# A two-layer hybrid decoder: ScalarE empties some PSUM banks alone, memory values in rows of 512, x transposed block by block in tasks of its own, another first block

## The chip, the cores and the metric

One core of a Trainium2 chip runs the whole program. TensorE (PE in the profile; PEld is its loading of the stationary operand) multiplies into PSUM banks; VectorE (DVE) and ScalarE (ACT) read PSUM and SBUF; GpSimd (POOL) does small work in SBUF; SyncE (SP) only issues DMAs here, one after another. Each engine works through its own instructions in the order in which they stand, and waits on semaphores for the others. The metric is the device time of one execution in microseconds (us), as a median over runs; lower is better.

## The reference

Two layers over x (512 tokens, 1024 wide), all in fp32, cut to its structure:

```python
for l in range(2):
    h = x @ w_in[l]                       # 1024 -> all branches' columns
    y_rwkv = rwkv7(...)                   # 8 heads x 64, delta-rule state, sequential
    q = rms(q_lat) @ w_uq; kv = rms(kv_lat) @ w_ukv
    y_mla = causal_attention(q, k, v) * silu(gate)          # 8 heads, 96 + 64 wide
    u = val * sigmoid(glu); u = causal_conv31(u) + conv_b
    y_conv = silu(layer_norm(u)) * silu(gate)
    kv = mem @ w_mem_kv                   # mem: 256 tokens; keys 512 wide, values 512 wide
    y_mem = attention(xq, k_mem, v_mem) * silu(gate)        # 4 heads x 128
    proj = [y_n @ w_o_branch[l, n] for n in range(4)]
    out = sum(sigmoid(x @ w_gate_n + b_n) * proj_n) @ w_out[l]
    x = layer_norm(alpha * x + out) * ln_g + ln_b
```

## The kernel before

**Three multiplications for one.** Every fp32 operand is split in two: `h`, the value rounded to TensorE's fp32r, and `lo`, the rest. `mm3` makes a product from lo·h, h·h and h·lo. `split(h, lo, src)` is a copy on ScalarE (h) and a subtraction on VectorE (lo), both reading `src`. Where `src` is a PSUM bank, the bank is held until VectorE has subtracted.

**Stages.** x stands transposed, as eight blocks of 128 features x 512 tokens (`xh`, `xl`). Per layer come the latents (`pl`, two items of 336 columns, `lat_item`), then blocks of 128 columns of W_in against all of x (`ps_glu`, `ps_val`, `ps_xq`, `ps_r` and so on, 24 multiplications of 128x512 each), causal attention in four pairs of heads (`pq` and `pk` project a pair, `heads` empties them and sends them by DMA to their places, `ms`, `mt`, `mo` are scores, transposes and sums), the memory attention (`ps_mk` keys, `pmv` values, `xs`, `xt`, `xo`), the convolution (31 taps on VectorE into `cacc`, then `conv_norm`), the RWKV chunks (64x64 multiplications `g`, `x`, `va`, `gb`, `w`, `yb`), and the merge (`ps_m` gates, `po` projections). At the end of layer 0 stand the output projection (`pz`), the LayerNorm per block of 128 tokens (`norm`, tiles `z` with statistics `lmv`, `lrs`, `lnb`), the store of x for later (`xtok`), and the transposes `xT` that make the next layer's x.

**What sets the order.** A planner (class `Plan`) runs when the program is built. It has a cost for each instruction, a clock for each engine, tasks (generators, each with a due time) and a stream of weight-consuming items. It lets a task issue when its time has come on TensorE's clock and otherwise the next piece of the stream; the instructions stand on each engine in the order in which it issued them. A change in one place therefore moves instructions in many others.

**Buffers.** `wr` holds 2 raw weight blocks (512 KB each), `wh`/`wl` 3 split ones; the DMA of a block is issued once the raw block two before it is split. PSUM has pools of 2 banks for projections (`pp`), 2 for transposes and small products (`pa`), 4 for the rest (`pg`).

**Between the layers.** `ORDER` lists the items: `z0` (512 columns of the output projection), `z2`, `z3` (256 each), `m0` to `m3` (keys of layer 1's memory) and `m4`, `m5` (its values, 256 columns each: 48 multiplications of 128x256). After the fourth `norm` one task goes over the eight blocks of x: four transposes into a `pa` bank, ScalarE's scale and shift into `xf`, ScalarE's copy `xh`, VectorE's `xl`; then the next block.

**The start.** SP issues x's block 0, the first two weight blocks, the other blocks of x. TensorE starts once block 0 of x and the whole first weight block are split, with the product that needs the latest part (`w0l`).

Of the kernel before, what the change touches and what calls it, by code (L numbers as in the profile page):

```python
# [24 lines left out]
U_SLOTS = 32  # L25
ORDER = ["z0", "m0", "m1", "z2", "m2", "m4", "z3", "m3", "m5"]
LOOK = 4
# [238 lines left out]
def trunk_kernel(ctx: ExitStack, tc: tile.TileContext, A, out, dbg=None):  # L266
# [163 lines left out]
    wlive = {"raw": 0, "hl": {}}  # L430

    def weights(name, src, parts, last=False):
# [29 lines left out]
        plan.spawn(run(), plan.done[raw.tensor.name][0])  # L462
        return ws

    def free(h):
        n = h.tensor.name
        wlive["hl"][n] -= 1
        if wlive["hl"][n] == 0:
            del wlive["hl"][n]

# [28 lines left out]
    def wide(get, ps, lhs, wait=None):  # L499

        for k in range(8):
# [3 lines left out]
            for b in range(len(ps)):  # L505
                xh, xl = lhs(k, b)
                mm3(ps[b], xh, xl, h, lo, k == 0, k == 7)
                if b % 2 and (k < 7 or b < 3):
                    yield
# [45 lines left out]
    def memory_items(l):  # L555
# [19 lines left out]

        def keep(x, i, b, ps):
            h, lo = (y[:, 256 * b:256 * b + 256] for y in res[x][i])
            return split(h, lo, ps)

        def keys(h):  # L580
            def run(get):
                ps = yield from project(get, ms, f"mk{h}_{l}", 256)
                yield from keep("k", h // 2, h % 2, ps)
                yield
            return run

        def vpart(b):
            def after(i, ps):
                yield from keep("v", i, b, ps)
                if b == i == 1:  # L590
                    MEM[l] = (res["k"], res["v"])
                yield

            def run(get):
# [4 lines left out]
        its += [([(A["w_mv"][l, b, kh], (512, 512)) for kh in range(2)], vpart(b)) for b in range(2)]  # L599
        return load, its, lambda: len(ms) == 8  # L600

    def layer_items(l):
# [28 lines left out]
        if l == 0:  # L631
            x0 = [u(f"x0{k}") for k in range(8)]
            DMA(x0[0], A["xT"][:, 0, :])

        def begin(get):
            if l == 0:
                def loads():
                    for k in range(1, 8):
                        if k == 4:
# [509 lines left out]
        def conv_norm():  # L1149
            ntok = []  # L1150
            yield lambda: added[3] == 8
            for tb in range(4):
                ps, = yield from pa.take([128, 512], f"ct{tb}" + t_)
                for i in range(4):
                    TR(ps[:, 128 * i:128 * i + 128], cacc[i][:, 128 * tb:128 * tb + 128])
                yield
                bs, mv = st(f"cbs{tb}" + t_, 6), st(f"cmv{tb}" + t_, 2)
                V.bn_stats(bs, ps)
                V.bn_aggr(mv, bs)
                rs = st(f"crs{tb}" + t_, 1)  # L1160
                rstd_of(rs, mv[:, 1:2], 1.0, LN_EPS)
                n = u(f"cn{tb}" + t_)
# [108 lines left out]
        def lat_item(nb):  # L1271
            def run(get):
# [5 lines left out]
                for k in range(8):  # L1278
                    h, lo = yield from get()
                    yield from part(X[l], k)  # L1280
                    for tb in range(4):
                        xh, xl = (x[:, 128 * tb:128 * tb + 128] for x in X[l][k])
                        mm3(ps[tb], xh, xl, h, lo, k == 0, k == 7)
                        if tb % 2:
                            yield
                    free(h)
# [346 lines left out]
        def end_items():  # L1633
# [148 lines left out]
            def norm(tb):  # L1782
# [31 lines left out]
                for k in range(8):  # L1814
                    ps, = yield from pa.take([128, 512], f"xT{k}" + t_)
                    plan.due(*[z[tb][k // 4] for tb in range(4)])
                    yield
                    for tb in range(4):
                        TR(ps[:, 128 * tb:128 * tb + 128], z[tb][k // 4][:, 128 * (k % 4):128 * (k % 4) + 128])
                    yield  # L1820
                    f = u(f"xf{k}" + t_)
                    h = xp.tile([128, 512], F32R, tag="xh", name=f"xh{k}_{l + 1}")
                    lo = xp.tile([128, 512], F32R, tag="xl", name=f"xl{k}_{l + 1}")
                    S.activation(f, ps, AF.Identity, scale=pr("ln_g", k), bias=pr("ln_b", k))
                    pa.free()
                    S.copy(h, f)
                    V.tensor_tensor(out=lo, in0=f, in1=h.bitcast(F32), op=ALU.subtract)
                    X[l + 1].append((h, lo))
                close_phase()
                closed[l] = True  # L1830

# [137 lines left out]
def layout(x, mem, positions, w_in, b_gate, rwkv_mu, rwkv_w0, rwkv_w2, rwkv_a0, rwkv_a2, rwkv_k_k, rwkv_k_a,  # L1969
# [29 lines left out]
    a["w_mk"] = np.stack([tiles(xattn_w_mem_kv[l][:, :512], 128, 8)[:, 0] for l in range(L)])  # L1999
    a["w_mv"] = np.stack([tiles(xattn_w_mem_kv[l][:, 512:], 256, 4) for l in range(L)])  # L2000
    a["w_o"] = np.stack([[tiles(w_o_branch[l, n], 128, 4)[:, 0].reshape(4, 2, 128, 512).transpose(0, 2, 1, 3).reshape(4, 128, 1024)
# [34 lines left out]
```

## Time and profile before

| | us |
|---|---|
| median of 3 runs (lowest, highest) | 1505.58 (1505.47, 1506.05) |
| profiled execution: its own time | 1506.66 |
| profiled execution: span of the core | 1504.9 |
| PE busy in the span | 1474.2 |
| DVE busy | 1053.5 |
| ACT busy | 662.1 |
| POOL busy | 137.1 |
| first multiplication starts, last one ends | 6.75, 1494.66 |
| mean granted TensorE clock over the span | 0.996 |

A busy engine is an engine with an instruction in flight; since multiplications overlap, PE busy says how long TensorE was occupied, not that it ran at its peak. Rows of a timeline have the start and length in us, the engine, the operation, what it writes and reads, and in brackets the idle time of the engine before it and what ended it.

### The profile page before, as it was taken

To read this page: it belongs to the slowest core of one execution; us is meant where nothing else is said; L and a number is where in the kernel's file an instruction comes from. 1 tells how busy PE (TensorE), PEld (TensorE's weight loads), DVE (VectorE), ACT (ScalarE), POOL (GpSimd) and SP (SyncE) were. 2 spreads that over 40 slices of the span, in tenths; PEclk is the share of its full clock that TensorE was granted. 3 is DMA by queue.
4 is the path that set the end of the run, shared out by engine and by line. 5 is a ranking of instruction groups with operands and counts; after the bars stand their busy time and mean duration, and the time that the engine had idled before them with its cause. 6 is when DMAs were issued, how large, how long until landed. Compare 5 with 4: busy or idle time off the path is not lost.

```text
span 1504.9 us, 29132 instructions
## 1 busy us (share of the span) xinstructions
PE 1474.2 (98%) x11896; PEld 1239.7 (82%) x11896; DVE 1053.5 (70%) x1994; ACT 662.1 (44%) x1270; POOL 137.1 (9%) x329
## 2 busy tenths in 40 slices
PE   8999999999999999999999999999999999999997
PEld 8888878888888888888998878888887788888886
DVE  5799997755757666645554888887876476757747
ACT  5546554434354543443255455533444344444332
POOL 0000000030303030000010000000030203021002
PEclk9999999999999999999999999999999999999998
DMA  6444333241322323434343252423332313233532
GB/s 213 124 136 108 86 100 96 84 111 59 86 83 78 91 74 95 136 103 129 114 147 108 82 138 68 116 92 99 88 95 72 97 47 107 63 107 116 165 99 70
DMA packets 89013, 153.50 MB, mean 102 GB/s; under 512 B 41008, under 2 KB 47152, under 8 KB 88880
## 3 DMA queue, kind: packets, MB, share of 16 engines
q1 hardware_dynamic: 88880, 151.65, 33.9%
q8 instruction: 93, 1.52, 0.4%
q14 instruction: 40, 0.33, 0.1%
HBM read 134.32 MB, written 5.77 MB: 93 GB/s over the span
## 4 chain that ended last, share of the span: by engine, by line
PE 90%; DVE 5%; ACT 2%; issue 1%; DMA 1%; POOL 0%; SPq 0%; ACTq 0%; POOLq 0%; DVEq 0%
PE ps_m L286 23%; PE po L286 11%; PE ps_xq L286 3%; PE ps_v L286 3%; PE ps_xg L286 3%; PE ps_cg L286 3%; PE ps_rg L286 3%; PE ps_k L286 3%; PE ps_mg L286 3%; PE ps_r L286 3%; PE ps_val L286 3%; PE ps_glu L286 2%; PE ms L286 2%; PE pl L286 2%; PE pz L286 2%; PE pmv L286 2%
## 5 line engine op out<-in xcount | busy, mean ns | idle before, releaser
L235 DVE SCALAR_TENSOR_TENSOR cacc<-hpad,prm,cacc 128x512 f32<-128x512 f32 x240 | 179.2, 749 | 3.9
L235 ACT ACTIVATE tm<-ps_m,prm 128x512 f32<-128x512 f32 x64 | 44.1, 689 | 166.6 <-PE ps_m L286 156.1
L235 DVE SCALAR_TENSOR_TENSOR mt<-tm,po 128x512 f32<-128x512 f32 x48 | 32.9, 686 | 89.9 <-PE po L286 89.6
L235 POOL TENSOR_TENSOR tmpW<-ZT,W 64x14 f32<-64x14 f32 (+6 forms) x112 | 42.7, 381 | 7.8
L235 POOL TENSOR_TENSOR ZT<-ZT,tmpW 64x14 f32<-64x14 f32 (+6 forms) x112 | 42.0, 375 | 8.8
L235 ACT ACTIVATE mP<-ms,nmm 128x128 f32<-128x128 f32 (+3 forms) x64 | 33.6, 529 | 20.3 <-DVE nmm L235 19.5
L235 POOL TENSOR_SCALAR ZT<-W 64x256 f32<-64x256 f32 x8 | 3.6, 447 | 369.7 <-DMA W<-scr 369.7
L235 ACT COPY mPT<-mt 128x128 f32<-128x128 f32 (+3 forms) x64 | 26.1, 428 | 19.6 <-PE mt L291 19.4
L235 DVE TENSOR_TENSOR merged<-merged,mt 128x512 f32<-128x512 f32 x48 | 33.6, 699 | 1.7
L235 POOL MEMSET D<- 128x8 f32 x8 | 0.9, 116 | 342.7 <-PE ms L286 321.2
L235 DVE TENSOR_REDUCE nmm<-ms 128x1 f32<-128x128 f32 (+3 forms) x64 | 30.0, 484 | 0.1
L235 POOL TENSOR_SCALAR lrs<-lmv 128x1 f32<-128x1 f32 x8 | 3.6, 447 | 253.6 <-DVE lmv L235 252.2
L235 DVE TENSOR_SCALAR mP<-mP,smm 128x128 f32<-128x128 f32 (+3 forms) x64 | 24.8, 387 | 2.3
L291 PE MATMUL mt<-cst,mP 128*128 128x128 f32 x160 | 25.9, 273 | 0.0
L235 DVE SCALAR_TENSOR_TENSOR merged<-tm,po 128x512 f32<-128x512 f32 x16 | 11.0, 687 | 20.1 <-PE po L286 20.0
L235 ACT ACTIVATE z<-z,lnb,lrs 128x256 f32<-128x256 f32 (+1 forms) x16 | 9.6, 647 | 30.1 <-DVE lnb L235 30.1
L235 POOL TENSOR_SCALAR gr<-gm 128x8 f32<-128x8 f32 x8 | 2.4, 298 | 224.0 <-DVE gm L235 224.0
L235 ACT ACTIVATE yb<-yb,mr,gr 128x64 f32<-128x64 f32 x64 | 22.1, 434 | 1.1 <-DVE mr L235 1.1
L286 PE MATMUL ms<-kTl,qT 96*128 96x128 f32 (+3 forms) x64 | 22.3, 348 | 0.0
L291 PEld LDWEIGHTS mt<-cst,mP 128*128 128x128 f32 x160 | 19.0, 141 | 3.6 <-ACT xP L235 0.2
L235 ACT ACTIVATE xP<-xs,nmx 128x256 f32<-128x256 f32 x32 | 15.1, 473 | 13.7 <-DVE nmx L235 11.2
L286 PE MATMUL ms<-kTh,qT 96*128 96x128 f32 (+3 forms) x64 | 20.6, 322 | 0.0
(3536 smaller groups left out, 5276.3 us busy)
## 6 DMA issues: line engine op xcount, KB each, us to landing
w<-in_w_ch_dram SPq DMA_DIRECT2D x146, 512.0 KB, 3.8
w<-in_w_o_dram SPq DMA_DIRECT2D x32, 512.0 KB, 3.7
w<-in_w_out_dram SPq DMA_DIRECT2D x16, 512.0 KB, 3.7
w<-in_w_lat_dram SPq DMA_DIRECT2D x16, 336.0 KB, 3.2
w<-in_w_mk_dram SPq DMA_DIRECT2D x8, 512.0 KB, 3.7
w<-in_w_mv_dram SPq DMA_DIRECT2D x8, 512.0 KB, 3.7
w<-in_w_qk_dram SPq DMA_DIRECT2D x8, 320.0 KB, 2.9
x<-in_xT_dram SPq DMA_DIRECT2D x8, 256.0 KB, 5.9
```

The costliest lines, as they stand in the source:

```text
L235: return self.plan.keep(f(*a, **k))
L286: plan.keep(nc.tensor.matmul(o, lhsT, rhs, start=start, stop=stop))
L291: plan.keep(nc.tensor.transpose(o, i, ident))
```

## The change

1. `ORDER` loses `m5`: the values of layer 1's memory are one item of 512 columns (`m4`) behind `z3` and `m3`; layer 0 has the same item. `w_mv` is laid out for it.
2. Eighteen multiplications of 128x256 on a constant (`warm`) stand first on TensorE; nothing reads them.
3. The first weight block comes in two DMAs and is split in two halves, and blocks 1 and 2 of x are issued ahead of the second weight block. For block 0 the products of the first four banks are issued h·h, then l·h, then h·lo.
4. `heads`: ScalarE copies the bank to SBUF with the scale; `split` then reads SBUF.
5. `conv_norm`: ScalarE copies the bank to SBUF, statistics and normalisation read that; the second affine is done on ScalarE.
6. Between the layers each block of x is a task of its own (`features`), so that two are under way in the two `pa` banks.

```diff
-ORDER = ["z0", "m0", "m1", "z2", "m2", "m4", "z3", "m3", "m5"]
+ORDER = ["z0", "m0", "m1", "z2", "m2", "z3", "m3", "m4"]
...
+    warm = pp.tile([128, 512], F32, tag="pp", name="warm")
+    for i in range(18):
+        MM(warm[:, 0:256], reset[:, 0:128], reset, start=True, stop=True)
...
-        DMA(raw, src)
+        first = name == "w0"
+        if first:
+            for i in range(2):
+                c = slice(parts[0] * i, parts[0] * i + parts[0])
+                DMA(raw[:, c], src[:, c], f"w0{i}")
+            for k in range(1, 3):
+                DMA(x0[k], A["xT"][:, k, :])
+        else:
+            DMA(raw, src)
...
-            if last:
+            if last or first:
                 for i, (w, c) in enumerate(zip(ws, parts)):
+                    if first:
+                        plan.t = max(plan.t, plan.done[f"w0{i}"][0])
+                        yield
...
-        def vpart(b):
...
-                return narrow(get, 256, 2, f"pmv{b}{l}", lambda k, i: [x[:, 128 * i:128 * i + 128] for x in ms[k]], after)
-            return run
+        def values(get):
+            ps = [pp.tile([128, 512], F32, tag="pp", name=f"pmv{i}_{l}") for i in range(1 + (l > 0))]
+            if l == 0:
+                ps += yield from pa.take([128, 512], f"pmv1_{l}")
+            yield from wide(get, ps, lambda k, b: [x[:, 128 * b:128 * b + 128] for x in ms[k]])
+
+            def after():
+                for i in range(2):
+                    yield from keep("v", i, slice(0, 512), ps[i])
+                if l == 0:
+                    pa.free()
+                MEM[l] = (res["k"], res["v"])
+            plan.spawn(after())
+            yield
...
                 yield
+                n = u(f"cn{tb}" + t_)
+                S.copy(n, ps)
+                pa.free()
                 bs, mv = st(f"cbs{tb}" + t_, 6), st(f"cmv{tb}" + t_, 2)
-                V.bn_stats(bs, ps)
+                V.bn_stats(bs, n)
...
-                V.tensor_scalar(out=n, in0=ps, scalar1=mv[:, 0:1], scalar2=rs, op0=ALU.subtract, op1=ALU.mult)
-                pa.free()
+                V.tensor_scalar(out=n, in0=n, scalar1=mv[:, 0:1], scalar2=rs, op0=ALU.subtract, op1=ALU.mult)
...
-                V.tensor_scalar(out=z, in0=ps, scalar1=pr("cln_g", i), scalar2=pr("cln_b", i), op0=ALU.mult, op1=ALU.add)
+                S.activation(z, ps, AF.Identity, scale=pr("cln_g", i), bias=pr("cln_b", i))
...
+                    if l == nb == k == 0:
+                        for a, b in ((0, h), (1, h), (0, lo)):
+                            for tb in range(4):
+                                MM(ps[tb], X[l][k][a][:, 128 * tb:128 * tb + 128], b, start=a == 0 and b is h, stop=False)
...
-            S.activation(parts[0], ps, AF.Copy, scale=s)
-            V.scalar_tensor_tensor(out=parts[1], in0=ps, scalar=s, in1=parts[0].bitcast(F32), op0=ALU.mult, op1=ALU.subtract)
+            raw = parts[1].bitcast(F32)
+            S.activation(raw, ps, AF.Copy, scale=s)
+            yield from split(*parts, raw)
...
+                    plan.spawn(features(k, [z[tb][k // 4][:, 128 * (k % 4):128 * (k % 4) + 128] for tb in range(4)]))
```

**How rows move.** First place: SP's queue at the start of the program (x00 to x07 are the blocks of x, w0 to w3 the first weight blocks). Before:

```order
L298 DMA x00_104<-in_xT_dram 128x512
L298 DMA w0_113<-in_w_lat_dram 128x672
L298 DMA w1_115<-in_w_lat_dram 128x672
L298 DMA x01_105<-in_xT_dram 128x512
L298 DMA x02_106<-in_xT_dram 128x512
L298 DMA x03_107<-in_xT_dram 128x512
```

and now:

```order
L298 DMA x00_123<-in_xT_dram 128x512
L298 DMA w0_132<-in_w_lat_dram 128x336 x2
L298 DMA x01_124<-in_xT_dram 128x512
L298 DMA x02_125<-in_xT_dram 128x512
L298 DMA w1_137<-in_w_lat_dram 128x672
L298 DMA x03_126<-in_xT_dram 128x512
```

The first weight block is two transfers, and the second one moved behind blocks 1 and 2 of x; x04 to x07, w2 and w3 follow as before.

Second place: ScalarE between the layers, behind the third token block's LayerNorm (`z20`). Before:

```order
L235 ACTIVATE z30_0_7314<-z30_0_7314,lnb3_0_8430,lrs3_0_8400 128x512
L235 CAST kmh1_1_7802<-ps_mk3_1_8406 128x256
L235 ACTIVATE xf0_0_8458<-xT0_0_8434,prm0_194 128x512
L235 CAST xh0_1_8459<-xf0_0_8458 128x512
L235 CAST w126h_8471<-w126_8407 128x1024
L235 ACTIVATE xf1_0_8479<-xT1_0_8464,prm0_194 128x512
L235 CAST xh1_1_8480<-xf1_0_8479 128x512
```

and now:

```order
L235 ACTIVATE z30_0_7296<-z30_0_7296,lnb3_0_8346,lrs3_0_8316 128x512
L235 CAST kmh1_1_7784<-ps_mk3_1_8322 128x256
L235 CAST w124h_8380<-w124_8323 128x1024
L235 ACTIVATE xf0_0_8383<-xT0_0_8368,prm0_224 128x512
L235 CAST xh0_1_8384<-xf0_0_8383 128x512
L235 ACTIVATE xf1_0_8388<-xT1_0_8369,prm0_224 128x512
L235 CAST xh1_1_8389<-xf1_0_8388 128x512
```

The copy `kmh1` of the last key bank still stands behind `z30`; w126, which was the second of the two last value blocks, is now the last of four (w123 to w126), and w124's copy stands ahead of x's first block.

Third place: ScalarE at the last pair of heads of layer 0 (`pq3`, `pk3` are its banks). Before:

```order
L235 CAST w34h_2226<-w34_2224 128x1024
L235 ACTIVATE xqh_0_2258<-pq3_0_2237 128x512
L235 ACTIVATE xP21_0_2202,smx211_0_2247<-xs21_0_2201,nmx211_0_2246 128x256
L235 CAST w35h_2271<-w35_2269 128x1024
L235 ACTIVATE xkh_0_2274<-pk3_0_2254 128x512
```

and now:

```order
L235 CAST w34h_2230<-w34_2228 128x1024
L235 COPY xy2_0_2262<-xo2_0_2253 128x512
L235 ACTIVATE xql_0_2269<-pq3_0_2241 128x512
L235 CAST xqh_0_2268<-xql_0_2269 128x512
L235 CAST w35h_2280<-w35_2278 128x1024
L235 ACTIVATE xkl_0_2284<-pk3_0_2264 128x512
L235 CAST xkh_0_2283<-xkl_0_2284 128x512
```

The bank is read by one ScalarE instruction (`xql<-pq3`), in the place where `xqh` stood; the copy behind it and VectorE's subtraction read SBUF.

More of the change, by code (lines that the diff above doesn't have):

```diff
@@ L460, in run @@
             wlive["raw"] -= 1
-        plan.spawn(run(), plan.done[raw.tensor.name][0])
+        plan.spawn(run(), plan.done["w00" if first else raw.tensor.name][0])
         return ws
@@ L507, in wide @@
                 mm3(ps[b], xh, xl, h, lo, k == 0, k == 7)
-                if b % 2 and (k < 7 or b < 3):
+                if b % 2 and (k < 7 or b < len(ps) - 1):
                     yield
@@ L574, in load, with keep @@
                     ms.append((h[:, c], lo[:, c]))
[L576 to L577 removed]
+        def keep(x, i, c, ps):
+            h, lo = (y[:, c] for y in res[x][i])
             return split(h, lo, ps)
@@ L582, in run @@
                 ps = yield from project(get, ms, f"mk{h}_{l}", 256)
-                yield from keep("k", h // 2, h % 2, ps)
+                yield from keep("k", h // 2, slice(256 * (h % 2), 256 * (h % 2) + 256), ps)
                 yield
             return run
-        def vpart(b):
[L588 to L594, printed above, removed]
-                return narrow(get, 256, 2, f"pmv{b}{l}", lambda k, i: [x[:, 128 * i:128 * i + 128] for x in ms[k]], after)
-            return run
+        def values(get):
[11 more added lines that the diff above has]
+            yield
         its = [([(A["w_mk"][l, h], (512, 512))], keys(h)) for h in range(4)]
-        its += [([(A["w_mv"][l, b, kh], (512, 512)) for kh in range(2)], vpart(b)) for b in range(2)]
+        its += [([(A["w_mv"][l, i], (512, 512)) for i in range(4)], values)]
         return load, its, lambda: len(ms) == 8
@@ L631, in layer_items @@
         if l == 0:
-            x0 = [u(f"x0{k}") for k in range(8)]
+            x0.extend(u(f"x0{k}") for k in range(8))
             DMA(x0[0], A["xT"][:, 0, :])
@@ L637, in loads @@
                 def loads():
-                    for k in range(1, 8):
+                    for k in range(3, 8):
                         if k == 4:
@@ L1814, in norm, with features @@
                 for k in range(8):
[L1815 to L1830, printed above, removed]
+                    plan.spawn(features(k, [z[tb][k // 4][:, 128 * (k % 4):128 * (k % 4) + 128] for tb in range(4)]))
+            def features(k, zs):
+                ps, = yield from pa.take([128, 512], f"xT{k}" + t_)
+                plan.due(*zs)
+                yield
+                for tb in range(4):
+                    TR(ps[:, 128 * tb:128 * tb + 128], zs[tb])
+                yield
+                f = u(f"xf{k}" + t_)
+                h = xp.tile([128, 512], F32R, tag="xh", name=f"xh{k}_{l + 1}")
+                lo = xp.tile([128, 512], F32R, tag="xl", name=f"xl{k}_{l + 1}")
+                S.activation(f, ps, AF.Identity, scale=pr("ln_g", k), bias=pr("ln_b", k))
+                pa.free()
+                yield from split(h, lo, f)
+                while len(X[l + 1]) < k:
+                    yield lambda: len(X[l + 1]) == k
+                X[l + 1].append((h, lo))
+                if k == 7:
+                    close_phase()
+                    closed[l] = True
             if l + 1 < LAYERS:
@@ L1999, in layout @@
     a["w_mk"] = np.stack([tiles(xattn_w_mem_kv[l][:, :512], 128, 8)[:, 0] for l in range(L)])
-    a["w_mv"] = np.stack([tiles(xattn_w_mem_kv[l][:, 512:], 256, 4) for l in range(L)])
+    a["w_mv"] = np.stack([tiles(xattn_w_mem_kv[l][:, 512:], 512, 2)[0] for l in range(L)])
     a["w_o"] = np.stack([[tiles(w_o_branch[l, n], 128, 4)[:, 0].reshape(4, 2, 128, 512).transpose(0, 2, 1, 3).reshape(4, 128, 1024)
```

22 lines of the change are left out of this document (13 added, 9 removed).

## The prediction

> **What bounds the kernel now.** I read the page's busy times and its chain of work that ended last, then the waits of TensorE, then the timeline at the places that the change touches.
>
> ```profile
> PE 1474.2 (98%) x11896; PEld 1239.7 (82%) x11896; DVE 1053.5 (70%) x1994; ACT 662.1 (44%) x1270; POOL 137.1 (9%) x329
> PE 90%; DVE 5%; ACT 2%; issue 1%; DMA 1%; POOL 0%; SPq 0%; ACTq 0%; POOLq 0%; DVEq 0%
> ```
>
> TensorE is busy for 98% of the span and carries 90% of the chain. So an edit can save time in three ways only: fewer or better shaped rows on TensorE, a higher clock for them, or a shorter wait of TensorE. Its waits, longest sum first (total us, times, longest), say how much there is:
>
> ```profile
> PE pl L286 <- DVE w0l L235: 6.7, 1, 6.7
> PE pmv L286 <- DVE w126l L235: 2.6, 1, 2.6
> PE tk L291 <- DVE S L235: 1.8, 1, 1.8
> PE pq L286 <- DVE xql L235: 1.6, 2, 0.9
> PE ps_xq L286 <- DVE xql L235: 1.4, 2, 0.9
> PE ps_glu L286 <- DVE xql L235: 1.1, 1, 1.1
> PE gb_0x L286 <- issue: 1.1, 1, 1.1
> ...
> PE ps_mg L286 <- DVE xql L235: 0.6, 1, 0.6
> PE gb_1x L286 <- issue: 0.6, 1, 0.6
> PE pz L286 <- DVE w123l L235: 0.6, 1, 0.6
> PE ps_val L286 <- DVE w11l L235: 0.5, 1, 0.5
> ```
>
> Three groups of these waits are edited: the head (w0l, 6.7), the heads' banks (xql, 1.6 + 1.4 + 1.1 + 0.6 = 4.7) and the place between the layers (w126l, w123l, 3.2). The other four rows (1.8 + 1.1 + 0.6 + 0.5 = 4.0) are not touched, but a re-planned order can move them.
>
> **The head.** Timeline and window of the start:
>
> ```profile
> 0.72 0.48 POOL L235 MEMSET reset<- 128x256 bf16 x2 [0.29 <-POOLq L2028]
> 5.05 0.75 ACT L235 CAST w0h<-w 128x672 fp32r<-128x672 f32 x1 [0.27 <-DMA w<-in_w_lat_dram]
> 6.75 0.65 PE L286 MATMUL pl<-w0l,xh 128*128 128x336 f32 x1 [6.75 <-DVE w0l L235]
> 11.67 0.48 PE L286 MATMUL pl_0x<-w0h,xl 128*128 128x336 f32 x1
> 12.37 0.32 PE L286 MATMUL pl_0xx<-w0h,xl 128*128 128x336 f32 x1
> 13.31 0.86 DVE L235 TENSOR_TENSOR w2l<-w,w2h 128x672 fp32r<-128x672 f32 x1 [0.35 <-ACT w2h L235]
> 16.65 0.31 PE L286 MATMUL pl<-w2l,xh 128*128 128x336 f32 x1
> 7.00:12.00 5.00, 5.00 (x19) 5.00 (x20) 4.23 (x7) 4.09 (x7) 0.00 (x0) 1.00 1.05 396
> ```
>
> TensorE starts at 6.75 and multiplies slowly (0.48 a piece) until about 12, 5.2 us after its start; then a piece takes 0.32. It reaches the fifth block of features, which needs w2, at 16.65, after 48 multiplications. The change acts twice. The h·h products need no lo part, and half of w0 is cast in half of 0.75, so the first multiplication can stand at 5.05 + 0.38, about 5.4, rather less since the half transfer lands sooner: I take 5.3. And the 18 dummy multiplications start when `reset` is written, at 0.72 + 0.48 = 1.2. If the clock again opens 5.2 us after the first work, it opens at 6.4, so some 4 of the 48 run slowly. By the starts of the pieces a slow one costs 0.28 and a fast one 0.153: 5.3 + 4 x 0.28 + 44 x 0.153 = 13.2. But w2 is split only at 13.31 + 0.86 = 14.17, and the window shows why it won't come sooner: the DMA engines are full (share 1.05, 396 GB/s) from 7 to 12, and the change adds no bytes and removes none. So w2 is the next to be late, and the gain is 16.65 - 14.2 = 2.45; less some for w1 behind two more blocks of x (0.5 MB, 1.3 us at 396 GB/s): **-2.3**. Bounds: -1.5 (those 1.3 us shown half) and -3.0 (w2's copy is also drawn forward by half of a split).
>
> The dummies cost nothing where TensorE waits anyway: 12 slow pieces of 256 columns took 2.75 us between the layers (row below), so 18 take 4.1 and end at 5.3. Without that cover they would cost up to 4.1.
>
> The Trainium skill, TensorE: Matmul & The Clock Gate, Part 1, puts the opening of the clock at about 3.4 us of sustained work, in a window that runs freely. By that rule it would open between 4.7 and 8.1, where this trace had 5.2 us of work; the end of the 48 multiplications would move by less than 0.8 us and stay ahead of w2, so the term is the same.
>
> **The values in rows of 512.** The chain has the old form and, in the latent values, the new one:
>
> ```profile
> 74.64 5.47 PE pv L286 x24
> 86.49 11.53 PE pmv L286 x96
> 769.68 2.75 PE pmv L286 x12
> 772.43 0.85 PE xT L291 x4
> 776.23 0.44 PE xT L291 x4
> ```
>
> 96 pieces of 256 columns took 11.53 (0.120 each), 24 pieces of 512 took 5.47 (0.228). A layer's 96 become 48: 48 x 0.228 = 10.94, a gain of 0.6 a layer: **-1.2** in both. Nothing waits behind it but the boundary, below.
>
> **The heads' banks.** At the fourth pair:
>
> ```profile
> 188.66 0.60 ACT L235 ACTIVATE xqh<-pq 128x512 fp32r<-128x512 f32 x1
> 190.39 0.68 DVE L235 SCALAR_TENSOR_TENSOR xql<-pq,xqh 128x512 fp32r<-128x512 f32 x1
> 191.12 0.50 PE L286 MATMUL ps_glu<-xl,w33h 128*128 128x512 f32 x1 [1.14 <-DVE xql L235]
> ```
>
> ScalarE had read the bank by 189.26, but VectorE's read ended at 191.07, because VectorE was working through its own queue, and TensorE waited 1.14 for it. In the change the only reader is the ScalarE instruction that ended at 189.26; TensorE would have gone on without a wait. The same holds for the five other waits on xql. The new copy (0.60 each, 16 of them) stands on ScalarE, busy for 44%. What it delays is the sending of the heads, by 0.6 a tile, and behind it the casts of weights; both have the projections of the next pair in front of them. Sum: 4.7 less 0.5 for places where ScalarE itself is late: **-4.2**; bounds -4.7 (all gone) and 0 (ScalarE's queue is as late as VectorE's was).
>
> **Between the layers.**
>
> ```profile
> 761.28 0.28 PE L286 MATMUL pz<-w123h,mg7l 128*128 128x256 f32 x1
> 764.77 0.81 ACT L235 ACTIVATE z<-z,lnb,lrs 128x512 f32<-128x512 f32 x1 [2.33 <-DVE lnb L235]
> 765.87 0.42 DVE L235 TENSOR_TENSOR kml<-ps_mk,kmh 128x256 fp32r<-128x256 f32 x1 [0.68 <-ACT kmh L235]
> 740.55 2.88 PE ps_mk L286 x24
> 766.00 0.78 ACT L235 ACTIVATE xf<-xT,prm 128x512 f32<-128x512 f32 x1 [0.16 <-PE xT L291]
> 766.51 0.60 PE L291 MATMUL xT<-cst,z 128*128 128x128 f32 x4
> 767.33 1.04 ACT L235 CAST w126h<-w 128x1024 fp32r<-128x1024 f32 x1
> 769.68 0.40 PE L286 MATMUL pmv<-w126l,memh 128*128 128x256 f32 x1 [2.57 <-DVE w126l L235]
> 766.00:773.00 7.00, 4.43 (x27) 4.19 (x25) 3.73 (x5) 4.67 (x7) 0.00 (x0) 0.78 0.70 232
> ```
>
> Lost before: 0.58 for w123, 2.57 for w126 (its cast stood between two blocks of x on ScalarE), and then a clock granted at 0.78 in the window: 12 pieces of `pmv` took 2.75 instead of 12 x 0.120 = 1.44, four `xT` 0.85 instead of 0.44, 1.7 together. Sum 4.9. In the change w126 is the last of four value blocks and its transfer has 8 us more of multiplications before it, so this wait goes. New is a wait for a bank: the second bank of the values was the last key bank, and its copy `kmh1` still stands behind `z30`. From the end of z3 (761.4) to the end of that subtraction (766.3) were 4.9 us; the keys now between them fill 2.88 and the first bank's three multiplications 0.68: 4.9 - 3.56 = 1.3 of waiting. Behind that bank's multiplications in TensorE's queue stand the transposes of x, which wait with them, and behind those the latents of the next layer. Then the blocks of x: two under way are drawn at ScalarE's pace (0.78 + the copy of x, some 0.6, a block) with casts of 1.04 among them, where the values cover most: 0.6 kept. Gain 4.9 - 1.3 - 0.6 = **-3.0**; bounds -4.9 and +0.3 (both new losses twice as large, and the clock's 1.7 stays, less the 0.3 that is w123's half).
>
> **At nothing:** `conv_norm` and the planner's other moves.
>
> ```profile
> L235 DVE TENSOR_SCALAR cn<-ct,cmv,crs 128x512 f32<-128x512 f32 x8 | 6.5, 810 | 7.9 <-POOL crs L235 7.9
> L235 ACT ACTIVATE xf<-xT,prm 128x512 f32<-128x512 f32 x8 | 6.2, 778 | 5.3 <-PE xT L291 5.3
> ```
>
> The affine goes from VectorE to ScalarE at about equal length, 8 copies come on ScalarE, and neither is in the chain there: projections run on TensorE meanwhile. If that cover were gone, eight copies of 0.6 are 4.8. The order changes everywhere, so the waits not edited, 4.0, may go or double: bounds ±4.0.
>
> **Sum:** -2.3 - 1.2 - 4.2 - 3.0 = -10.7. The profiled execution took 1506.66 (its span 1504.9 and 1.8 around it), which gives 1496.0; the median of the runs shown, 1505.58, lies 1.1 below it, so 1494.9. I forecast **1495.0**.
>
> **Rivals.**
>
> *The clock closes between the layers as before.* For: 1.3 of waiting and eight transposes (2 x 0.44) stand close together. Against: 3.2 us without multiplications closed it before (766.51 to 769.68), here it is 2.2, and the two parts have three multiplications between them. Price: the 1.7 above: 1496.7. (The Trainium skill, TensorE: Matmul & The Clock Gate, Part 4, says that transposes don't count as busy for the clock, and Part 1 that an idle window of about 3.4 us closes it. By these two the 2.2 us are all idle for the gate, but too short; no row here tells transposes apart from waiting.)
>
> *The heads' waits move to ScalarE's queue.* The bank is free when ScalarE comes to it, and ScalarE now has twice the work per bank and casts of 1.04 that themselves wait for weights. For: ScalarE's place is as much the planner's guess as VectorE's was. Against: its idle share of 56%, and the row at 188.66. Price: the whole 4.2, and 0.8 of the rest: 1500.
>
> *No change that can be measured.* The head's gain is lost because the weights behind w2 bind the next stage at the rate of DMA (full from 7 to 12), and the boundary waits for x at ScalarE's pace: 2.3 + 3.0 + 4.2 given back leaves 1.2, and one lost wait as long as the longest untouched one (1.8) takes it: 1505.6. For: DMA's share of 1.05. Against: it is far lower in the page's later slices, and of all weight blocks only w11, w123 and w126 stand among TensorE's waits.
>
> *Slower.* The attention's chain gets longer: two more ScalarE copies of 0.60 per pair before the heads can be sent, 8 pairs in the program, 9.6 us, if scores wait for the heads in each pair, while the heads' 4.2 stay as waits: 1494.9 + 4.2 + 9.6 = 1508.7. It decides from the point where the last pair's scores run out of other multiplications. Against: between a pair's projection and its scores stand projections of 24 pieces, about 5.5 us by the row of 24, and TensorE now waits for no score.
>
> **How the numbers follow.** Chances: forecast 0.60 (own range 1489 to 1500), clock 0.06, ScalarE's queue 0.12, no change 0.09, slower 0.13. A measurement of this kernel can tell about 0.2%, 3 us, from no change: faster is 0.60 + 0.06 + 0.12 = 0.78, within 0.09, slower 0.13. The range reaches from 1489 (all bounds that lower the time, half used) to 1505, which leaves out the slower case, half of the no-change case and little at the low end.
>
> **What would show it.** Head: the first real multiplication at 5.3, pieces of 0.32 from about 7, and w2's first at 14.2. Heads: no wait of TensorE on xql above 0.3, or a wait on ScalarE in its place. Boundary: a wait of `pmv` for `kml` of 1.3 in place of w126l's 2.6, and a granted clock near 1.0. Values: 48 pieces of 0.228. Wrong it would be if waits of `ms` or `mt` for heads appear, or if the sum of TensorE's waits stays above 15 us.

## The result and the profile after

| | before | changed |
|---|---|---|
| median (lowest to highest), us | 1505.53 (1505.01 to 1506.05), 4 runs | 1492.34 (1491.31 to 1492.70), 4 runs |
| profiled execution: own time, span | 1506.66, 1504.9 | 1492.32, 1490.5 |

The ratio is 0.9911 (95% interval 0.9894 to 0.9928): 13.2 us faster in the medians, 14.3 between the two profiled executions.

The page of the changed kernel, busy times and chain:

```profile
PE 1472.6 (99%) x11818; PEld 1233.5 (83%) x11818; DVE 1044.7 (70%) x1983; ACT 678.5 (46%) x1299; POOL 141.4 (9%) x329
PE 89%; DVE 5%; DMA 2%; ACT 1%; POOL 1%; issue 1%; SPq 0%; ACTq 0%; DVEq 0%; POOLq 0%
```

TensorE is busy 1.6 us less although 4.0 us of dummies came, and ScalarE 16 us more. What the change bought is seen in TensorE's waits (total us, times, longest):

```profile
PE tk L291 <- DVE S L235: 1.8, 1, 1.8
PE warm L286 <- POOL reset L235: 1.3, 1, 1.3
PE pmv L286 <- DVE kml L235: 1.2, 1, 1.2
PE pl L286 <- DVE w0l L235: 0.9, 1, 0.9
PE po L286 <- DVE merged L235: 0.8, 1, 0.8
PE ps_val L286 <- DVE w11l L235: 0.5, 1, 0.5
```

No row names xql, w123l or w126l any more, and no issue. The row of `kml` is the new wait that the prediction had named.

To place the gain I worked out a table from the traces: the time of a stage less the sum of its multiplications at their usual pace. (The pace of a shape is the median distance between starts in the profile of before, for the 64-wide shapes the mean.) What is left is waiting, slow clock and switching between shapes. The 1.2 us that the values gain by their shape is not in it.

| stage | before | before, again | changed |
|---|---|---|---|
| to the first real multiplication | 6.75 | 6.64 | 4.94 |
| to the fifth block of x | 2.56 | 2.33 | 2.75 |
| to the first `pq` of layer 0 | 1.13 | 1.09 | 1.19 |
| attention of layer 0 (to its last `mo`) | 7.30 | 7.38 | 4.37 |
| RWKV and merge of layer 0 (to the first `pz`) | 7.70 | 7.68 | 8.29 |
| between the layers (to the first `ps_glu` of layer 1) | 6.03 | 6.05 | 2.22 |
| attention of layer 1 | 5.87 | 5.87 | 3.82 |
| RWKV and merge of layer 1 (to the last multiplication) | 13.12 | 12.39 | 9.82 |
| sum | 50.5 | 49.4 | 37.4 |

The difference of the sums, 13.1, and the 1.2 make the 14.3. The same places of the timeline as before, first the head:

```profile
1.26 4.02 PE L286 MATMUL warm<-reset 128*128 128x256 bf16 x18 [1.26 <-POOL reset L235]
4.94 0.63 PE L286 MATMUL pl<-w0h,xh 128*128 128x336 f32 x1
7.07 0.62 ACT L235 CAST xh<-x 128x512 fp32r<-128x512 f32 x1 [2.22 <-DMA x<-in_xT_dram]
7.60 0.47 ACT L235 CAST w0h<-w 128x336 fp32r<-128x336 f32 x1
8.89 0.42 PE L286 MATMUL pl<-w0l,xh 128*128 128x336 f32 x1 [0.89 <-DVE w0l L235]
13.33 0.75 ACT L235 CAST w2h<-w 128x672 fp32r<-128x672 f32 x1 [0.24 <-DMA w<-in_w_lat_dram]
15.03 0.42 PE L286 MATMUL pl<-w2l,xh 128*128 128x336 f32 x1 [0.21 <-DVE w2l L235]
```

Two things are new: a wait at 8.89 (the second half of w0, landed at 5.14, stands in ScalarE's queue behind the cast of a block of x that landed at 7.05), and w2 cast at 13.33, not at 12.52 as before.

The fourth pair of heads:

```profile
187.60 0.60 ACT L235 ACTIVATE xql<-pq 128x512 f32<-128x512 f32 x1
188.23 0.62 ACT L235 CAST xqh<-xql 128x512 fp32r<-128x512 f32 x1
188.27 0.48 PE L286 MATMUL ps_glu<-xl,w33h 128*128 128x512 f32 x1
189.03 0.68 DVE L235 TENSOR_TENSOR xql<-xql,xqh 128x512 fp32r<-128x512 f32 x1
```

TensorE writes the bank at 188.27, just behind ScalarE's one read; VectorE's subtraction at 189.03 no longer matters to it.

Between the layers, with a window behind it:

```profile
753.61 0.81 ACT L235 ACTIVATE z<-z,lnb,lrs 128x512 f32<-128x512 f32 x1 [2.33 <-DVE lnb L235]
754.33 0.35 ACT L235 CAST kmh<-ps_mk 128x256 fp32r<-128x256 f32 x1
754.71 0.42 DVE L235 TENSOR_TENSOR kml<-ps_mk,kmh 128x256 fp32r<-128x256 f32 x1 [0.68 <-ACT kmh L235]
755.19 0.50 PE L286 MATMUL pmv<-w123l,memh 128*128 128x512 f32 x1 [1.21 <-DVE kml L235]
755.00:762.00 7.00, 6.81 (x38) 5.71 (x39) 3.73 (x6) 6.32 (x9) 0.00 (x0) 1.00 0.75 266
```

The wait for the bank is there, 1.21 for the 1.3 worked out, and the granted clock stays at 1.00 where it was 0.78.

### The profile page after: what moved, and what is told of

It is laid out like the page before. It is cut to its first block, busy times and chain, and to the rows that moved or that the text cites. A ratio compares the mean times of both kernels' runs of the same rounds, so it can differ in the third digit from the quotient of the medians.

```text
span 1490.5 us, 28989 instructions
## 1 busy us (share of the span) xinstructions
PE 1472.6 (99%) x11818; PEld 1233.5 (83%) x11818; DVE 1044.7 (70%) x1983; ACT 678.5 (46%) x1299; POOL 141.4 (9%) x329
## 4 chain that ended last, share of the span: by engine, by line
PE 89%; DVE 5%; DMA 2%; ACT 1%; POOL 1%; issue 1%; SPq 0%; ACTq 0%; DVEq 0%; POOLq 0%
PE ps_m L286 24%; PE po L286 12%; PE ps_cg L286 3%; PE ps_xg L286 3%; PE ps_xq L286 3%; PE ps_rg L286 3%; PE ps_mg L286 3%; PE ps_v L286 3%; PE ps_val L286 3%; PE ps_r L286 2%; PE ps_glu L286 2%; PE ps_k L286 2%; PE pz L286 2%; PE ms L286 2%; PE pl L286 2%; PE x L286 1%
## 5 line engine op out<-in xcount | busy, mean ns | idle before, releaser
L235 POOL TENSOR_TENSOR ZT<-ZT,tmpW 64x14 f32<-64x14 f32 (+6 forms) x112 | 38.6, 344 | 8.8
L235 ACT ACTIVATE xP<-xs,nmx 128x256 f32<-128x256 f32 x32 | 15.2, 475 | 12.1 <-DVE nmx L235 8.3
```

The lines of the kernel that those rows point to most:

```text
L235: return self.plan.keep(f(*a, **k))
```

## The experiments

Times are medians (lowest to highest). The kernels before that ran beside them had medians from 1505.7 to 1506.3.

| kernel | us | what is different |
|---|---|---|
| u_bank | 1499.99 (1499.34 to 1502.95) | changed, VectorE reads the heads' bank again |
| u_feat | 1492.97 (1492.19 to 1493.39) | changed, x one block after another |
| u_values | 1498.20 (1497.20 to 1498.80) | changed, old order of items and values of 256 columns |
| u_conv | 1498.24 (1497.09 to 1499.42) | changed, old `conv_norm` |
| c_due | 1494.36 (1493.65 to 1494.95) | u_conv, normalisation issued when its statistics are due |
| b_heads | 1504.09 (1501.50 to 1508.63) | before, with the heads' edit |
| before_again | 1505.64, 1 run | the kernel before |
| u_warm | 1494.34 (1493.11 to 1494.77) | changed, no dummies |
| u_first | 1492.11 (1491.06 to 1493.58) | changed, first block in one load |
| o_m3 | 1494.21 (1492.28 to 1496.72) | changed, last keys ahead of z3 |
| nd_fill | 1491.90 (1491.49 to 1492.54) | changed, kmh1 ahead of z30, dummies in the second block's wait |
| nd_first | 1490.35 (1490.13 to 1490.63) | u_first, kmh1 ahead of z30 |

**Who holds the heads' bank (u_bank).**

```diff
             raw = parts[1].bitcast(F32)
             S.activation(raw, ps, AF.Copy, scale=s)
-            yield from split(*parts, raw)
+            S.copy(parts[0], raw)
+            yield
+            V.scalar_tensor_tensor(out=parts[1], in0=ps, scalar=s, in1=parts[0].bitcast(F32), op0=ALU.mult, op1=ALU.subtract)
```

> The changed kernel, but VectorE's subtraction for the heads reads the PSUM bank again (ScalarE's two instructions stay). If the bank's release by ScalarE is what took the heads' waits away, TensorE waits on xql again, 3 to 5 us in sum, and the time is 1495.5 to 1498 against 1492.3. Rival (the waits went because the planner put things elsewhere, not because of the reader): no such waits, 1491.5 to 1493.5.

TensorE's waits in u_bank:

```profile
PE pq L286 <- DVE xql L235: 2.3, 2, 1.5
PE ps_xq L286 <- DVE xql L235: 1.7, 2, 1.0
PE ps_glu L286 <- DVE xql L235: 1.1, 1, 1.1
PE ps_val L286 <- DVE xql L235: 0.8, 1, 0.8
```

The waits are back, 5.9 in sum; the two attention stages lose 8.2 and 6.9 us (4.4 and 3.8 in the changed kernel). The same two instructions stand on ScalarE in both, so it is the reader of the bank that counts. The time went 2 us past the expected range. VectorE's read now stands behind two ScalarE instructions, where the kernel before had one, and the waits are longer than its 4.7; so u_bank is not quite the old form. The profile is of the longest run (1502.95): there the head and the last RWKV stage lost 1.8 and 2.1 more, each with a stretch of slow clock, of which more below.

**The heads' edit alone (b_heads).** The edit of the heads put into the kernel before.

> The kernel before with the heads' edit alone. If the heads' waits are cut by the bank's earlier release whatever the rest does: all six waits of TensorE on xql (4.7) gone, 1500 to 1501.5, attention stages at 4.4 and 3.8 of loss as in the changed kernel. Rival (it takes the planner's other new places too): some of the waits stay, 1502.5 or more.

The heads' part came as expected: attention loses 4.5 and 3.7, as in the changed kernel. Of TensorE's waits for a pair's bank one of 0.9 is left, on ScalarE. But the time is only 1504.1, with runs from 1501.5 to 1508.6, and the ratio to before, 0.9991 (95% interval 0.9981 to 1.0001), is not clear of no change. The profile is of one of the longest runs (1508.60). There the gain is given back in the RWKV stage of layer 0, which loses 14.5 instead of 7.7. The timeline and windows there:

```profile
390.78 1.22 DVE L235 TENSOR_TENSOR w65l<-w,w65h 128x1024 fp32r<-128x1024 f32 x1
391.92 0.69 DVE L235 BATCH_NORM_STATS2 cbs<-ct 128x6 f32<-128x512 f32 x1
392.64 0.18 DVE L235 BATCH_NORM_AGGREGATE cmv<-cbs 128x2 f32<-128x6 f32 x1
393.77 0.81 DVE L235 TENSOR_SCALAR cn<-ct,cmv,crs 128x512 f32<-128x512 f32 x1 [0.94 <-POOL crs L235]
394.49 0.68 DVE L235 SCALAR_TENSOR_TENSOR mt<-tm,po 128x512 f32<-128x512 f32 x1
395.23 0.79 PE L286 MATMUL ps_r<-xl,w64h 128*128 128x512 f32 x1 [2.93 <-DVE mt L235]
395.00:398.00 3.00, 2.77 (x7) 2.20 (x8) 2.93 (x5) 1.05 (x1) 1.06 (x3) 0.50 0.55 198
398.00:401.00 3.00, 3.00 (x9) 2.32 (x8) 2.55 (x5) 0.42 (x1) 2.45 (x8) 0.50 0.44 139
```

VectorE stands still for 0.94 at `cn`, since `crs` comes from GpSimd. Behind `cn` in VectorE's queue stands `mt`, which empties a bank of `po` that TensorE had written by 389.6. Ahead of it stand w65's lo part (1.22), the block's statistics, the 0.94 of standing and `cn` itself (0.81), so VectorE comes to it at 394.49. TensorE waits 2.93 for it, and then the granted clock is 0.50 for 6.8 us. By estimate the wait, and half of those 6.8, make 6.3 of the 6.8 that the stage loses more. All of this but w65's lo part is the convolution's work, which the prediction had at nothing. The clock fell twice more in this profile, for 3.4 us each, at 773 (as in the kernel before) and at 1200. The mean clock of the runs goes roughly with their times, from 0.993 in the two of 1508.6 to 0.998 in the one of 1501.5; so the spread looks like the clock's, though only one of the eleven has a trace.

**The convolution (u_conv, c_due).** The change has two more lines in `conv_norm` than its description shows: `plan.due(rs)` and a `yield` ahead of the normalisation, so that the planner issues it when its statistics are due. u_conv puts all the old lines of `conv_norm` back, without these two; c_due is u_conv and

```diff
+                plan.due(rs)
+                yield
                 n = u(f"cn{tb}" + t_)
                 V.tensor_scalar(out=n, in0=ps, scalar1=mv[:, 0:1], scalar2=rs, op0=ALU.subtract, op1=ALU.mult)
```

> The changed kernel with conv_norm as before (VectorE reads the banks and does the second affine). The changed kernel lost 3.3 us less in layer 1's RWKV stage than before, which the prediction had at nothing. If that is the planner's new order and not conv_norm, the time stays within 1.5 us of 1492.3 and the stage's loss moves by any sign. Rival (VectorE's relief in conv_norm is the cause): the stage loses some 3 us again, 1495 to 1496.

u_conv is 5.9 us slower than the changed kernel, beyond both readings. The loss is for the most part not in layer 1 (10.9 for 9.8) but in layer 0's RWKV stage: 13.5 for 8.3, with a wait of `ps_r` for `mt` of 2.9, at the same instructions as in b_heads, and a clock of 0.50 for 3.4 us behind it.

> The kernel u_conv (conv_norm on VectorE as before) with one thing more: the normalisation is issued only when its statistics are due, as in the changed kernel. If the 5.9 us of u_conv came from VectorE standing still for GpSimd's statistics with the merge's product queued behind (0.94 per block, then 2.9 of TensorE's waiting for a bank), that wait goes and the time falls to 1492 to 1494. Rival (VectorE reading the banks is too much work for it at this place): 1497 to 1498.5 as u_conv.

The groups of `cn` in u_conv and in c_due:

```profile
L235 DVE TENSOR_SCALAR cn<-ct,cmv,crs 128x512 f32<-128x512 f32 x8 | 6.5, 810 | 7.9 <-POOL crs L235 7.9
```

```profile
L235 DVE TENSOR_SCALAR cn<-ct,cmv,crs 128x512 f32<-128x512 f32 x8 | 6.5, 806 | 1.6 <-POOL crs L235 1.6
```

VectorE's standing falls from 7.9 to 1.6, TensorE's wait for `mt` goes, the stage is back at 8.7; the time, 1494.4, is 0.4 above the expected range. The rows of VectorE in c_due at this place:

```profile
386.77 0.69 DVE L235 SCALAR_TENSOR_TENSOR mt<-tm,po 128x512 f32<-128x512 f32 x1 [0.73 <-PE po L286]
388.11 1.22 DVE L235 TENSOR_TENSOR w65l<-w,w65h 128x1024 fp32r<-128x1024 f32 x1
389.24 0.81 DVE L235 TENSOR_SCALAR cn<-ct,cmv,crs 128x512 f32<-128x512 f32 x1
```

The `mt` of the first `po` now stands ahead of both `cn` and w65's lo part. So the two lines act by the order that the planner makes of them; the 0.94 of standing is only a part of what stood ahead of `mt`. Of the 5.9 they give 3.9; who reads the bank, and who does the affine, is in the other 2.0, of which the table by stage shows 1.3. The kernel before has the same standing (7.9) and no such wait of TensorE: there `mt` stands behind `cn` too, but ahead of w65's lo part (392.12 and 393.45), and TensorE still has twelve multiplications of `po` to do, until 395.11, before it needs the bank.

**The values and the order of items (u_values).** `ORDER`, `values` and the layout of `w_mv` as before; the blocks of x stay spread.

> The changed kernel with the old order of items and values in rows of 256 (m4 and m5). By the prediction: 0.7 and 0.6 for the rows, the wait for w126 (2.6) and the slow clock (1.7) back, the wait of pmv for kml (1.2) gone: +4.4, 1496.7. Rival (only the shape of the rows matters, since the transposes are spread now): +1.3, 1493.6, no wait above 1 us between the layers.

5.9 slower. 3.4 are between the layers (5.66 for 2.22), 1.2 the shape, 2.8 in layer 1's RWKV stage, where 2.2 of waits named issue stand; the attention of layer 0 loses 1.1 less and its RWKV stage 0.4 less. The wait between the layers changed its name:

```profile
763.57 1.04 ACT L235 CAST w126h<-w 128x1024 fp32r<-128x1024 f32 x1
765.35 1.11 PE L291 MATMUL xT<-cst,z 128*128 128x128 f32 x4 [1.61 <-ACT xf L235]
765.00:768.00 3.00, 2.65 (x13) 2.66 (x14) 2.26 (x4) 2.94 (x6) 0.00 (x0) 0.51 0.35 77
```

The cast of w126 stands between two blocks of x on ScalarE again; with two blocks under way it is the transposes that wait (0.6 and 1.6) and not `pmv`, and the clock goes to 0.51 all the same. So the trace puts the gain on the later place of w126, as the prediction had it; no run moves that alone.

**x block by block (u_feat).**

```diff
-                for k in range(8):
-                    plan.spawn(features(k, [z[tb][k // 4][:, 128 * (k % 4):128 * (k % 4) + 128] for tb in range(4)]))
+                def blocks():
+                    for k in range(8):
+                        yield from features(k, [z[tb][k // 4][:, 128 * (k % 4):128 * (k % 4) + 128] for tb in range(4)])
+                plan.spawn(blocks())
```

> The changed kernel with the eight blocks of x in one task, one block after another, as before. If the gain between the layers comes from w126's later place and the clock, as the prediction has it, two blocks at a time are worth little: 1492.3 to 1493.3. Rival (the pair of blocks under way is what keeps TensorE fed): waits at xT or at the first pl on x return, 1494.5 or more.

0.6 slower, which the runs cannot tell from nothing; the stage itself loses less (1.68 for 2.22). Two blocks at a time give nothing here.

**What in the head counts (u_warm, u_first).** u_warm leaves the dummies out; u_first has w0 in one load, x's blocks behind w1, and the old order of products, with the dummies.

> The changed kernel without the eighteen dummy multiplications. First real multiplication at 4.9 again; the clock would open some 5.2 us after it, at 10.1 instead of 7. If the second half of w0 (8.9) and w2 (15.0) bound the start, as the trace of the changed kernel has it, the fifth block of features starts only 0.2 to 0.6 later: 1492.5 to 1493. Rival (the clock bounds the start): each slow step costs its 0.127, 12 to 20 of them, 1.5 to 2.5 us: 1494 to 1495.

> The changed kernel with the first weight block in one load, x's blocks behind the second one, and the product order of before; the dummies stay. The first multiplication returns to 6.7. If w2's arrival is what binds and the split load delays it (w0's raw buffer is free at 8.8 in the changed kernel, 6.7 before), the fifth block starts at 14.2 to 14.6, and the time is 1491.5 to 1492.3: the first block in two loads gains nothing. Rival (the early first product is what the head gained): the fifth block starts at 16 to 16.7, 1493.3 to 1494.

Starts of the blocks of x in the first item, from the traces (us), with the number of slow steps (0.25 to 0.35 from start to start) among the first 48:

| | first | second | third | fifth | slow steps |
|---|---|---|---|---|---|
| before | 6.75 | 10.27 | 12.98 | 16.65 | 18 |
| changed | 4.94 | 8.89 | 10.86 | 15.03 | 8 |
| u_warm | 4.78 | 9.59 | 13.12 | 16.88 | 21 |
| u_first | 6.55 | 9.23 | 11.60 | 15.28 | 3 |
| nd_first | 6.71 | 8.66 | 10.49 | 14.18 | 1 |

My expectation for u_warm failed: no run of it is as fast as any of the changed kernel, 2.0 us in the medians. Its clock opens only behind the second block, which takes 3.5 us for the changed kernel's 2.0, and the fifth block starts at 16.88. That of u_first held in the time: without the split the first multiplication is 1.6 later and the time is the same, though its fifth block started at 15.28 and not by 14.6. So the dummies are the head's whole gain in these runs; the early first product is taken back by the wait for the second block. Without the dummies it gains nothing either: the fifth block of u_warm is no earlier than that of the kernel before.

**The wait at the second block costs a clock.** In the profiles of u_bank and o_m3, whose heads are the changed kernel's, the fifth block started at 16.84 and 16.71. Windows of o_m3 and of u_bank:

```profile
10.00:13.00 3.00, 3.00 (x13) 3.00 (x12) 3.00 (x6) 2.81 (x6) 0.00 (x0) 0.50 0.94 307
```

```profile
11.00:15.00 4.00, 4.00 (x18) 4.00 (x17) 3.71 (x7) 3.49 (x6) 0.00 (x0) 0.57 0.93 309
```

There the wait for w0's second half was 1.9 and 2.6, and the clock closed behind it; with waits of 0.9, and with 1.8 in u_conv, it did not. How long the wait is hangs on two things. One is the transfers at the start: x's second block landed at 7.7 and 7.8 in these two, at 7.05 in the changed kernel's profile. The other is when the clock opened, and with it the end of the first block: in u_conv x landed at 6.99, but the clock had opened at 4.8 and the first block ended at 7.0 (7.1 and 8.0 in the changed kernel), so TensorE waited longer.

The clock records of the fourteen traces show what goes with it. In each execution the clock changes only at the ends of periods of 3.41 us (in the kernel before it stayed open for 757.76, which is 222 of them), and the periods lie elsewhere in each execution. Every period at full clock in which TensorE had no multiplication in flight for 1.85 us or more was followed by a slow one; none with 1.73 or less was. The wait in o_m3 lay in one period, and 1.85 of the 2.6 in u_bank did; the 1.8 of u_conv fell on two periods, 1.24 and 0.58. Between the two bounds stand nine periods with 1.75 or 1.76: all hold the wait of `tk` in layer 1's RWKV stage, which is in every kernel, and the clock closed behind it in u_bank and b_heads alone. This is a count over the traces; no run was made to test it.

**Attempts at the wait for kml (o_m3, nd_fill, nd_first).**

```diff
-ORDER = ["z0", "m0", "m1", "z2", "m2", "z3", "m3", "m4"]
+ORDER = ["z0", "m0", "m1", "z2", "m2", "m3", "z3", "m4"]
```

> The changed kernel with the last key block ahead of the last quarter of the output projection (z2, m2, m3, z3, m4). The bank that pmv waits for is then emptied 2.9 us earlier: the wait on kml (1.2) goes, and the transposes of x come 2.9 us later behind z3 with 10.9 us of values to cover them: 1490.8 to 1491.6. Rival (x's blocks become the late ones, the first pl of layer 1 waits for x): 1492.3 or more.

A miss: the wait on kml went, and a wait of 1.6 came ahead of z3, for a weight block that the keys' time had covered:

```profile
746.31 0.39 PE L286 MATMUL pz<-w122l,mg4h 128*128 128x256 f32 x1 [1.56 <-DVE w122l L235]
```

The stage loses 2.58 for 2.22; the rest of the 1.9 by which it is slower is the head in its profile, where the fifth block started 1.7 later. nd_fill and nd_first make ScalarE come to the key bank before it waits for the LayerNorm's factor:

```diff
+                plan.due(nb)
+                yield
                 S.activation(z[tb][0], z[tb][0], AF.Identity, scale=rs, bias=nb)
```

nd_fill adds eight dummies behind the first block of x, nd_first takes the first block of u_first.

> The changed kernel with two additions. One: the LayerNorm's scaling between the layers is issued when its factor is due, so that kmh1 stands ahead of z30 on ScalarE: the wait of pmv for kml falls from 1.2 to 0.2, that stage's loss from 2.2 to 1.2. Two: eight dummy multiplications between the first and the second block of x, in TensorE's wait of 0.9 to 2.6: the clock stays at 1.0 from 8 to 15 us and the fifth block starts at 15.0 in this execution too, not at 16.7 to 16.8 as in two of the profiles. Time 1490.8 to 1491.6, and no run above 1492.5. Rival (the dummies only push the second block back, by 0.5 to 0.9): 1492 or more.

> The same addition between the layers, with the first weight block in one load as in u_first. Same stage loss between the layers, 1.2. If the split of the first block gains nothing, it is level with the kernel with dummies in the wait: 1490.6 to 1491.8. Rival (the split helps once the clock stays open): 0.5 us or more slower than that one.

In nd_first:

```profile
752.03 0.37 ACT L235 CAST kmh<-ps_mk 128x256 fp32r<-128x256 f32 x1 [2.47 <-PE ps_mk L286]
752.43 0.42 DVE L235 TENSOR_TENSOR kml<-ps_mk,kmh 128x256 fp32r<-128x256 f32 x1
752.91 0.50 PE L286 MATMUL pmv<-w123l,memh 128*128 128x512 f32 x1
```

The wait on kml is gone in both; the stage loses 1.55 and 1.57, some 0.65 less than the changed kernel and not the 1.0 expected, since a wait of `xT` of 0.4 is new. nd_fill held its clock (3 slow steps) but its fifth block started at 15.29, no earlier than in the changed kernel: 1491.9, which is 0.3 above the expected range and no clear gain. nd_first, expected level with nd_fill, is 1.5 faster. It is the fastest kernel of the study, 1490.35, ratio to before 0.9897 (0.9884 to 0.9911); each of its runs is below each of the changed kernel, and its four runs lie within 0.5 us. Of the 2.0 us by which it beats the changed kernel 0.65 are this wait and 0.85 the head of its profile (fifth block at 14.18 for 15.03); since u_first, with the same head, had 15.28, part of that may be how the transfers fell (x's last block at 11.3 and 12.5).

**The kernel before, again (before_again).**

> The kernel before once more, to see what of its waits belongs to the program. The waits on VectorE and on weights should stand at the same instructions with the same lengths. The waits named issue (1.1 at gb_0x, 0.6 at gb_1x in layer 1): if they belong to the program they stand there again; rival: they belong to one execution, and stand elsewhere or not at all, up to 2 us of the 3.3 gained in layer 1's RWKV stage being chance.

The waits named issue are at the same two instructions, 0.7 at gb_0x and 0.5 at gb_1x, so they belong to the program. They went with the planner's new order, and came back with another one in u_values. What makes them was not found.

## Why the prediction was right, point by point

The sign, the range and the size were right: 1495.0 forecast, 1492.3 measured. Of the 14.3 between the profiles 11.6 are in the places that the prediction named, where it had 10.7; the other 2.7 are in places that it put at nothing, and that part of the gain is luck. The low end of its range does not follow from its words: the lower bounds of the terms add up to 7.1 below the forecast, and half of that gives 1491.5, not 1489; 1492.3 lies above both. By its own steps:

- **Head, -2.3: mis-sized, and for a partly wrong reason.** The fifth block started 1.6 earlier. The step that failed is that w2 comes no later because no bytes are added: it was cast 0.8 later. The last block of x ahead of it already landed later: with w0 in two loads between 12.1 and 13.1 in nine profiles, with one load between 11.3 and 11.7 in four and at 12.5 in u_first. That goes with the split and its order of transfers; how was not found. It is not that w2's transfer was issued later (8.87 for 6.72, since its buffer is w0's): before and now it landed 0.9 behind the last block of x. Of the two parts of the edit the forecast gave the early product its due and the dummies only cover. By u_warm and u_first it is the other way round: dummies 2.0, split 0.
- **Values, -1.2: right.** Layer 0's values took 10.90 in 48 pieces, 11.51 in 96 before.
- **Heads, -4.2: right, somewhat low.** All six waits on xql are gone, and nothing of note came on ScalarE in their place; the two stages gained 2.9 and 2.05. u_bank shows the bank's reader as the cause. In the kernel before the edit alone is not clear of no change (b_heads), since other waits came with it. The rival that the waits move to ScalarE's queue fell: 0.2 to 0.5 at one `pq` in some kernels. The slower case fell too: no score waited for the heads longer.
- **Between the layers, -3.0: right, 0.8 low.** The wait for kml was 1.2 for 1.3, w126's wait and the slow clock went. The 0.6 kept for ScalarE's pace did not show. The rival of the clock closing here did not happen.
- **`conv_norm` at nothing: wrong, though inside its bounds.** The cover that the prediction named, projections on TensorE, is there, but they need a bank that VectorE empties behind `cn`. Without this edit the heads' gain is lost again: in b_heads wholly in the profiled run, in u_conv 5.9. In the difference between before and changed it shows as nothing, since before did not pay for its standing. Its worth here is that it keeps the heads' gain, and the larger part, 3.9 of 5.9, is when the normalisation is issued (c_due), not who reads the bank, which is what the prediction weighed.
- **Other moves, 0 within 4.0:** layer 0's RWKV stage lost 0.6, layer 1's gained 3.3 (2.6 against the second profile of before). 1.7 and 1.2 of that are the issue waits, the rest is spread over switches between shapes and was not traced.

## What to carry to other kernels

Where TensorE waits for a PSUM bank, look at which engine reads it last and what stands ahead of that read in its queue: a single read by the engine with the shorter queue took away six waits of 0.6 to 1.1 us here, even at the price of one more copy. An instruction that waits for a third engine holds everything behind it, so it should be issued when its operand is due; such a stall may cost nothing until another edit puts a bank's reader behind it and more work ahead. Test the parts of an edit both ways, taken out of the new kernel and put into the old one: the heads' edit looked worth 7.7 us by the one, where the way back was not quite the old form, and by the other 2.0 (1504.1 beside 1506.1), which those runs cannot tell from nothing.

## What the runs showed of the hardware that I had not expected

A wait of TensorE of 2 to 3 us can cost more than itself, since the granted clock fell to 0.50 behind it: for 3.4 us behind 1.9 in o_m3, 2.6 in u_bank and before, 2.9 in u_conv, and for 6.8 behind 2.9 in b_heads. By estimate such a stretch of 3.4 at half the clock costs TensorE 1.7 where it is busy. The length of the wait alone does not say whether it happens: 1.8 at the head of u_conv and 1.2 between the layers went by without it, and the wait of `tk` for `S`, 1.5 to 1.8 in every trace, was followed by it in two of fourteen. What went with it is how much of one period of 3.41 us stood idle, 1.85 or more; where two waits of 0.6 and 1.6 stand 2.3 apart (u_values), they add up to 1.95 in one period, and the clock fell too. Since the periods lie elsewhere in each execution, the same kernel may or may not pay for such a wait. The Trainium skill, TensorE: Matmul & The Clock Gate, Part 1, puts the idle window at about 3.4 us, running freely; the traces agree with the length and with the free running, but here waits well below that were followed by a slow clock, and the measurement decides.
